# A two-layer diffusion backbone on one core: the adaLN rows and columns of the first stage issued one block ahead, and a residual moved within the change of layers

## The chip, the cores and the metric

The kernel runs on one core of a Trainium2 chip. The metric is the device time of one execution in microseconds (us). Engines are called as in the profile: PE is TensorE's matmul, PEld its weight load, DVE is VectorE, ACT ScalarE, POOL GpSimd, SP the engine whose queue issues the DMAs.

## The reference

512 latent tokens and 256 context tokens of width 1024 pass through two layers with an inner width of 2048. Layer 0 mixes tokens by a gated linear recurrence in both directions (five projections: q, two forget gates, v, and the gate z), layer 1 by a Fourier transform over tokens and over groups of channels. Each layer normalizes its input, scales and shifts it by columns computed from a condition vector (adaLN), and adds its result, times a gate, to the stream.

```python
def adaln(cvec, w, b):
    m = jax.nn.silu(cvec) @ w + b
    return jnp.split(m, 3, axis=-1)

def reference(x, c, ctx, c_ctx, ada_w, ada_b, norm_g, ...):
    x_lat, x_ctx = x, ctx
    for i in range(DEPTH):
        sh_l, sc_l, gt_l = adaln(c, ada_w[i], ada_b[i])
        h_lat = rms_norm(x_lat, norm_g[i]) * (1.0 + sc_l[:, None]) + sh_l[:, None]
        if i % N_MIXERS == 0:
            sh_c, sc_c, gt_c = adaln(c_ctx, ada_w[i], ada_b[i])
            h_ctx = rms_norm(x_ctx, norm_g[i]) * (1.0 + sc_c) + sh_c
            lb = hgrn_lower_bound(hg_lb_logits, j)
            y_lat, y_ctx = hgrn_mixer(h_ctx, h_lat, hg_w_in[j], lb, hg_norm_g[j], hg_w_out[j], ctx_out)
        else:
            y_lat = fourier_mixer(h_lat, ft_w_in[j], ft_w_out[j])
        x_lat = x_lat + gt_l[:, None] * y_lat
    return rms_norm(x_lat, final_g)
```

## The kernel before

All products are fp32 products made of two halves: `split` (L55 to L57) copies the rounded high half on ACT and subtracts it on DVE for the low half, and `mm3` (L95 to L97) is a triple of matmuls, high by high, high by low, low by high. `W` is the stream of weights: `W.loaded(n)` issues the DMA of weight block n (`wr`, 512 KB), `W.halves(n)` splits it into `wh` and `wl` (block 3 into `wz`). All large DMAs stand in SP's queue, in which a DMA is issued when the one eight places earlier has landed.

The first stage writes its order for PE, ACT and DVE by hand (`manual_schedule`). It goes over eight blocks d of 128 model columns:

- `ada_mm(d)` makes the adaLN rows: `rp` (L213, two weight tiles `wa`), then ACT copies them to `row` (L215).
- `ada_cols(d)` turns them into columns: `mp` (L221), then DVE makes `acol` and `bcol` (L222, L224).
- `turn(d, e)` transposes the normalized tokens into `tp` (L232), e = 0 for the latent tokens, e = 1 for the context.
- `modulate(d, e)` applies the columns to `tp`: the high half `hlh` (context `hc`) on ACT (L238), the full value `h32` on ACT (L241) or DVE (L243), the low half `hll` (context `hc`) on DVE (L245).
- `product(j, k)` is the triple of the projection j with block k; `first` is the sum in PSUM. Projections 0 to 2 run inside the latent loop, projection 3 in the loop over the context blocks that closes the stage.
- `square` and `normalize` prepare the tokens; `lower_bounds` makes a small matmul (`lp`) for the gates; `keep_warm` issues matmuls whose result nobody reads.

Behind that stage a scheduler sets the order from the program's text: context gates `pfc` first, then the projections, the recurrence and the output projection. At the change of layers `out0_late` makes the last output matmuls (`o0a`), tile m of 128 tokens by tile; `tail0(n)` adds token tile n's residual (`res`, `x`, L771 and L772), squares and sums (L778, L780), takes the reciprocal root on POOL (`rstd`, L179 and L180), builds a diagonal matrix of it (`dg`, L787) and the normalized halves `xn` (L788, L789). `turn1(d, r)` transposes and normalizes by a matmul with `dg` (`h1t`, L795) and makes the halves `h1h` and `h1l` (L797 to L804) for token tiles 0 and 1 (r = 0) or 2 and 3 (r = 1). `table` and `channel_table` split the Fourier tables (`tab`, `dft`). Then come the first gate products `ze` and the Fourier products `hp`.

Of the kernel before, what the change touches and what calls it, by code (L numbers as in the profile page):

```python
# [16 lines left out]
KT = D // P  # L17
T = 512
NT = T // P
TC = 256  # L20
NTC = TC // P
# [6 lines left out]
def view(t, off, dims):  # L28
    return bass.AP(t.tensor, t.offset + off, [t.ap[0]] + dims)
# [3 lines left out]
def hgrn_fourier_kernel(ctx: ExitStack, tc: tile.TileContext, a):  # L33
# [15 lines left out]
    def psG(name):  # L49
        return psum("G", 2, name)  # L50
# [60 lines left out]
    def ada_load(d):  # L111
        wa[d] = []
        for j in range(2):
            h = KT // 2
            if d < 4:
                w = py.tile([P, h, 256], F32, tag=f"yp{2 * d + j}", name=f"wa{d}_{j}")
            else:
                w = p0.tile([P, h, 256], F32, name=f"wa{d}_{j}")
            nc.sync.dma_start(out=w, in_=a["ada_a"][d][:, j * h:(j + 1) * h, :])
            wa[d].append(w)  # L120
# [14 lines left out]
    def keep_warm(n, name):  # L135
        wp = psG(name)
        for j in range(n):
            pe.matmul(wp, ones_r, view(ones_r, 0, [[0, 4], [1, P]]), start=True, stop=True)
# [64 lines left out]
    def normalize(n):  # L203
        rst = rstd_of(ss[:, n:n + 1], 1, D, p0, f"x{n}")
        v.tensor_scalar(out=xs[:, n, :], in0=xs[:, n, :], scalar1=rst, scalar2=None, op0=ALU.mult)
# [3 lines left out]
    def ada_mm(d):  # L209
        rp = psM(f"rp{d}")  # L210
        for k in range(KT):
            j = 32 * (k % 4)
            pe.matmul(rp[j:j + 32, :256], spad[:, k, :], wa[d][k // 4][:, k % 4, :], start=(k < 4), stop=(k >= 4))  # L213
        row = p0.tile([P, 256], F32, tag="row", name=f"row{d}", bufs=2)
        s.activation(row, rp[:, :256], AF.Copy)  # L215
        mcol[d] = row

    def ada_cols(d):
        mp = psM(f"mp{d}")
        for h in range(2):  # L220
            pe.matmul(mp[:, h * 2:h * 2 + 2], mcol[d][:, h * P:(h + 1) * P], sel, start=True, stop=True)  # L221
        v.tensor_scalar(out=acol[:, d, :], in0=mp[:, 2:4], scalar1=bp1[:, 8 + d:9 + d],  # L222
                        scalar2=vcol[:, 48 + d:49 + d], op0=ALU.add, op1=ALU.mult)
        v.tensor_scalar(out=bcol[:, d, :], in0=mp[:, 0:2], scalar1=vcol[:, 16 + d:17 + d], scalar2=None, op0=ALU.add)  # L224
# [3 lines left out]
    def turn(d, e):  # L228
        n0, n1 = ((0, NT), (NT, NT + NTC))[e]
        tp = turned[d, e] = psG(f"tp{d}_{e}")  # L230
        for n in range(n0, n1):
            pe.transpose(tp[:, (n - n0) * P:(n - n0 + 1) * P], xs[:, n, d * P:(d + 1) * P], ident)  # L232

    def modulate(d, e):
        n0, n1, th, tl = ((0, NT, *hlat), (NT, NT + NTC, *hctx))[e]
        w = (n1 - n0) * P
        tp = turned[d, e]
        s.activation(th[d], tp[:, :w], AF.Identity, scale=acol[:, d, e:e + 1], bias=bcol[:, d, e:e + 1])  # L238
        h32 = p0.tile([P, T], F32, tag="h32", name=f"h32_{d}_{e}", bufs=2)
        if e == 0 and d % 2:  # L240
            s.activation(h32[:, :w], tp[:, :w], AF.Identity, scale=acol[:, d, e:e + 1], bias=bcol[:, d, e:e + 1])  # L241
        else:
            v.tensor_scalar(out=h32[:, :w], in0=tp[:, :w], scalar1=acol[:, d, e:e + 1], scalar2=bcol[:, d, e:e + 1],  # L243
                            op0=ALU.mult, op1=ALU.add)
        v.tensor_tensor(out=tl[d], in0=h32[:, :w], in1=th[d].bitcast(F32), op=ALU.subtract)  # L245
# [47 lines left out]
    W = Weights(specs)  # L293
    FIRST = (1, 2, 0, 3)
    with tc.manual_schedule(engines={mybir.EngineType.PE, mybir.EngineType.Activation, mybir.EngineType.DVE}):
        first = {}

        def product(j, k):
            st = FIRST[j]
            if k == 0:  # L300
                first[st] = psP(f"first{st}")
            mm3(first[st], W.parts[j][0][:, k, :], W.parts[j][1][:, k, :], hlh[:, k, :], hll[:, k, :], k == 0, k == KT - 1)

        W.loaded(0)
        ada_load(1)
        ada_load(2)
        W.loaded(1)
        ada_load(3)
        ada_load(4)
        W.loaded(2)  # L310
        for d in range(5, KT):
            ada_load(d)
        W.loaded(3)
        for n in range(NTC):
            nc.sync.dma_start(out=xs[:, NT + n, :], in_=a["ctx"][n * P:(n + 1) * P, :])
        keep_warm(24, "warm1")
        for n in range(NT):
            square(n)
        for n in range(NT):
            normalize(n)  # L320
        ada_mm(0)
        keep_warm(3, "warm2")
        todo = {2: [(0, 0), (1, 0)], 3: [(0, 1), (1, 1), (2, 0), (2, 1)]}
        for d in range(KT):
            if d > 0:
                ada_mm(d)
            if d == 5:
                lower_bounds()
            turn(d, 0)
            if d == 0:  # L330
                keep_warm(4, "warm3")
            for j, k in todo.get(d, [(j, d - 2) for j in range(3)] if d > 3 else []):
                product(j, k)
            if d == KT - 1:
                for n in range(NT, NT + NTC):
                    square(n)
            ada_cols(d)
            modulate(d, 0)
            if d < 3:
                W.halves(d)  # L340
            if d == 6:
                W.halves(3)
        for j in range(3):
            product(j, KT - 2)
        for n in range(NT, NT + NTC):
            normalize(n)
        for j in range(3):
            product(j, KT - 1)
        for d in range(2):
            turn(d, 1)  # L350
        for d in range(KT):
            modulate(d, 1)
            product(3, d)
            if d + 2 < KT:
                turn(d + 2, 1)
# [310 lines left out]
    LAST = 13  # L666
# [12 lines left out]
    def out0_step(k, y2, w, m, hf, first, last):  # L679
        c, cm = slice(hf * 512, hf * 512 + 512), slice((m % 2) * P, (m % 2) * P + P)  # L680
        mm3(acc_of(m, hf), y2[:, 0, cm], y2[:, 1, cm], w[0][:, c], w[1][:, c], first, last)
# [10 lines left out]
    def out0_late():  # L692
        for k in range(LAST, 16):
            w = W.get(at["o0", 0, k])
            for r in range(2):
                y2 = y_parts(k, r)
                for m in (2 * r, 2 * r + 1):
                    for hf in range(2):
                        out0_step(k, y2, w, m, hf, r == 1 and k == LAST, r == 0 and k == 15)
            yield  # L700
        held = []
        for k in range(LAST):
            held.append((k, y_parts(k, 1), W.get(at["o0", 1, k])))
            if k == LAST - 2:
                continue
            for m, hfs in ((2, (0, 1)), (3, (0,)), (3, (1,))) if k == LAST - 1 else ((2, (0, 1)), (3, (0, 1))):
                for kk, y2, w in held:
                    for hf in hfs:
                        out0_step(kk, y2, w, m, hf, False, kk == LAST - 1)
            held = []  # L710
            yield

# [44 lines left out]
    def table(n):  # L757
        traw = pw.tile([P, 2, NF], F32, tag="wr", name=f"traw{n}")
        nc.sync.dma_start(out=traw, in_=a["tab"][:, n])
        tab = fp.tile([P, 2, 2, NF], F32R, tag=f"tb{n}", name=f"tab{n}")  # L760
        split(tab[:, :, 0, :], tab[:, :, 1, :], traw)
        tabs.append(tab)
# [20 lines left out]
    def tail0(n, acc):  # L783
        residual(n, acc)
        r = sum_sq(ss1, n, x1[:, n, :], f"x1_{n}")
        dg[n] = fp.tile([P, P], F32, tag="dg", name=f"dg{n}", bufs=2)
        v.tensor_scalar(out=dg[n], in0=ident, scalar1=r, scalar2=None, op0=ALU.mult)  # L787
        s.activation(xn[n][0], x1[:, n, :], AF.Copy, scale=r)  # L788
        v.scalar_tensor_tensor(out=xn[n][1], in0=x1[:, n, :], scalar=r, in1=xn[n][0].bitcast(F32),  # L789
                               op0=ALU.mult, op1=ALU.subtract)  # L790
# [22 lines left out]
    def acc_row(m):  # L813
        return [acc0[m, hf] for hf in range(2)]

    for k, _ in enumerate(out0_late()):
        if k in (3, 5):
            tail0(k // 2 - 1, acc_row(k // 2 - 1))
        if 7 <= k < 15:
            turn1(k - 7, 0)  # L820
        if k in (11, 12, 13):
            table(k - 11)
    table(3)
    channel_table()
    for n in range(2, 4):
        tail0(n, acc_row(n))


    zs_of = {}
# [66 lines left out]
    for b in range(2):  # L896
        m = fp.tile([1, NG // 2, NF], F32, tag=f"tb{b}", name=f"mid{b}")
# [139 lines left out]
```

## Time and profile before

| | us |
|---|---|
| median of 3 runs | 1208.31 (1207.48 to 1209.96) |
| the profiled execution | 1207.37, of which its span 1205.6 |
| TensorE busy | 1183.0 |
| VectorE, ScalarE, GpSimd busy | 763.1, 563.7, 43.0 |
| mean granted TensorE clock | 0.995 |

Times in a profile row count from the start of the span; the first number is the start, the second the duration, and in brackets stands the idle time of that engine ahead of it and what ended it. Matmuls overlap, so the step from one row's start to the next is what a matmul costs in a row of them. In a windows row the clock behind the busy times is the one that the throttle granted, 1.00 being full.

### The profile page before, as it was taken

The page shows a single profiled execution, that of the slowest core. Times are in us where ns is not written, and L with a number is a line of the kernel's source. Part 1 is how long each engine was busy: PE and PEld are TensorE (multiplying, and loading weights), DVE is VectorE, ACT ScalarE, POOL GpSimd, SP SyncE. Part 2 cuts the span into 40 slices and gives each one's busy share as a digit, 9 for nine tenths or more (in the row PEclk, how much of TensorE's full clock was granted, in tenths as well). Part 3 has the DMA queues.
Part 4 walks back from the last instruction along what each step waited for, and adds up shares of the span by engine and source line. Part 5 has one row for each costly group of instructions (what it writes and reads, how often), then busy time and mean ns, then how long its engine had stood idle before and what let it go on. Part 6 is the DMA issues. An engine that isn't in the chain of part 4 may idle for free.

```text
span 1205.6 us, 19232 instructions
## 1 busy us (share of the span) xinstructions
PE 1183.0 (98%) x7805; PEld 1043.4 (87%) x7805; DVE 763.1 (63%) x1250; ACT 563.7 (47%) x1130; POOL 43.0 (4%) x76
## 2 busy tenths in 40 slices
PE   7899999999999999999999999999999999999997
PEld 5699899899889889989988988998888998988885
DVE  5486655575765775686457547458576856668554
ACT  4355544554454453445445455355556533333322
POOL 2100000000000000000000000000000000000000
PEclk9999999999999999999999999999999999999998
DMA  9434211122510521242121112113545313333221
GB/s 352 177 122 156 71 54 53 53 71 70 161 61 29 182 77 54 69 142 71 36 70 54 36 54 69 37 53 109 175 168 184 110 42 134 106 108 119 88 88 70
DMA packets 33674, 118.54 MB, mean 98 GB/s; under 512 B 3879, under 2 KB 4144, under 8 KB 33586
## 3 DMA queue, kind: packets, MB, share of 16 engines
q1 hardware_dynamic: 33586, 117.32, 28.6%
q8 instruction: 61, 1.00, 0.3%
q14 instruction: 27, 0.22, 0.1%
HBM read 115.20 MB, written 2.10 MB: 97 GB/s over the span
## 4 chain that ended last, share of the span: by engine, by line
PE 91%; DVE 4%; DMA 2%; ACT 1%; issue 1%; POOL 0%; SPq 0%; DVEq 0%; POOLq 0%; ACTq 0%
PE gp L584 6%; PE pq L95 4%; PE pq L97 4%; PE pq L96 4%; PE pf L95 4%; PE pf L97 4%; PE pf L96 4%; PE vps L95 4%; PE vps L96 4%; PE vps L97 4%; PE pfc L95 2%; PE pfc L96 2%; PE pfc L97 2%; PE o0a L97 2%; PE o0a L95 2%; PE o0a L96 2%
## 5 line engine op out<-in xcount | busy, mean ns | idle before, releaser
L56 ACT ACTIVATE wh<-wr 128x1024 fp32r<-128x1024 f32 x140 | 147.9, 1058 | 225.8 <-PE pq L96 88.3
L57 DVE TENSOR_TENSOR wl<-wr,wh 128x1024 fp32r<-128x1024 f32 x140 | 170.8, 1220 | 103.6 <-ACT wh L56 101.9
L592 DVE TENSOR_TENSOR z<-z,tt 128x512 f32<-128x512 f32 x192 | 124.1, 688 | 120.6 <-PE gp L584 94.4
L95 PE MATMUL pf<-hlh,wh 128*128 128x512 f32 x240 | 99.3, 414 | 0.0
L95 PE MATMUL pq<-hlh,wh 128*128 128x512 f32 x240 | 96.9, 404 | 0.0
L545 ACT ACTIVATE kk<-z 128x512 f32<-128x512 f32 x96 | 61.8, 643 | 71.8 <-DVE z L592 71.6
L97 PE MATMUL pf<-hlh,wl 128*128 128x512 f32 x240 | 94.5, 394 | 0.0
L97 PE MATMUL pq<-hlh,wl 128*128 128x512 f32 x240 | 93.9, 391 | 0.0
L96 PE MATMUL pf<-hll,wh 128*128 128x512 f32 x240 | 93.8, 391 | 0.0
L96 PE MATMUL pq<-hll,wh 128*128 128x512 f32 x240 | 93.6, 390 | 0.0
L584 PE MATMUL gp<-z,kk 128*128 128x128 f32 x640 | 86.1, 277 | 0.6 <-ACT kk L545 0.6
L584 PEld LDWEIGHTS gp<-z,kk 128*128 128x128 f32 x640 | 81.4, 191 | 4.3 <-ACT kk L545 1.5
L95 PE MATMUL pfc<-hc,wh 128*128 128x256 f32 x256 | 74.8, 292 | 0.0
L95 PE MATMUL vps<-wh,hlh 128*128 128x256 f32 x256 | 74.2, 290 | 0.0
L97 PE MATMUL vps<-wh,hll 128*128 128x256 f32 x256 | 72.5, 283 | 0.0
L96 PE MATMUL vps<-wl,hlh 128*128 128x256 f32 x256 | 72.5, 283 | 0.0
L96 PE MATMUL pfc<-hc,wh 128*128 128x256 f32 x256 | 72.4, 283 | 0.0
L97 PE MATMUL pfc<-hc,wl 128*128 128x256 f32 x256 | 72.4, 283 | 0.0
L97 PEld LDWEIGHTS pf<-hlh,wl 128*128 128x128 f32 x240 | 45.0, 188 | 10.4 <-issue 0.2
L97 PEld LDWEIGHTS pq<-hlh,wl 128*128 128x128 f32 x240 | 45.0, 188 | 9.9
L95 PEld LDWEIGHTS pf<-hlh,wh 128*128 128x128 f32 x240 | 45.2, 188 | 9.6 <-issue 1.9
L96 PEld LDWEIGHTS pf<-hll,wh 128*128 128x128 f32 x240 | 45.3, 189 | 8.1 <-issue 0.2
(270 smaller groups left out, 3013.3 us busy)
## 6 DMA issues: line engine op xcount, KB each, us to landing
wr<-hg_w SPq DMA_DIRECT2D x64, 512.0 KB, 3.6
ar<-ada_r SPq DMA_DIRECT2D x32, 512.0 KB, 3.8
wr<-ft_w SPq DMA_DIRECT2D x32, 512.0 KB, 3.6
wr<-hg_wout SPq DMA_DIRECT2D x29, 512.0 KB, 3.4
wa<-ada_a SPq DMA_DIRECT2D x16, 512.0 KB, 10.5
wr<-hg_v SPq DMA_DIRECT2D x16, 512.0 KB, 3.4
wr<-ft_wout SPq DMA_DIRECT2D x16, 512.0 KB, 3.4
xs<-x SPq DMA_DIRECT2D x4, 512.0 KB, 3.6
```

The lines of the kernel that those rows point to most:

```text
L56: s.activation(hi, src, AF.Copy)
L57: v.tensor_tensor(out=lo, in0=src, in1=hi.bitcast(F32), op=ALU.subtract)
L95: pe.matmul(out, lh, rh, start=first, stop=False)
L96: pe.matmul(out, lh, rl, start=False, stop=False)
L97: pe.matmul(out, ll, rh, start=False, stop=last)
L545: s.activation(view(kk, 0, [[2 * h, T // (2 * h)], [h, 2], [1, h]]), view(z4, 2 * T, [[2 * h, T // (2 * h)], [T + h, 2], [1, h]]), AF.Copy)
L584: pe.matmul(gp[:, n * P:(n + 1) * P], kk[:, n * P:(n + 1) * P], view(z4, n * P, dims), start=True, stop=True)
L592: v.tensor_tensor(out=za, in0=za, in1=ta, op=ALU.mult)
```

## The change

In the first stage, `ada_mm` and `ada_cols` of block d + 1 are issued in block d; the first weight block is split ahead of `ada_mm(0)`; the triples are spread in another way over the blocks; weight block 3 and the context are loaded ahead of the adaLN weights of blocks 6 and 7, split or squared in block 5 and normalized in block 6; weight block 4 is split within the context loop at d = 3; the context's `h32` of odd blocks goes to ACT. At the change of layers `tail0(2)` stands directly behind the last matmuls of token tile 2, and `tail0(3)` ahead of the tables.

```diff
--- before.py
+++ after.py
@@ -237,7 +237,7 @@
         tp = turned[d, e]
         s.activation(th[d], tp[:, :w], AF.Identity, scale=acol[:, d, e:e + 1], bias=bcol[:, d, e:e + 1])
         h32 = p0.tile([P, T], F32, tag="h32", name=f"h32_{d}_{e}", bufs=2)
-        if e == 0 and d % 2:
+        if d % 2:
             s.activation(h32[:, :w], tp[:, :w], AF.Identity, scale=acol[:, d, e:e + 1], bias=bcol[:, d, e:e + 1])
         else:
             v.tensor_scalar(out=h32[:, :w], in0=tp[:, :w], scalar1=acol[:, d, e:e + 1], scalar2=bcol[:, d, e:e + 1],
@@ -308,48 +308,54 @@
         ada_load(3)
         ada_load(4)
         W.loaded(2)
-        for d in range(5, KT):
-            ada_load(d)
+        ada_load(5)
         W.loaded(3)
         for n in range(NTC):
             nc.sync.dma_start(out=xs[:, NT + n, :], in_=a["ctx"][n * P:(n + 1) * P, :])
+        for d in range(6, KT):
+            ada_load(d)
         keep_warm(24, "warm1")
         for n in range(NT):
             square(n)
         for n in range(NT):
             normalize(n)
+        W.halves(0)
         ada_mm(0)
         keep_warm(3, "warm2")
-        todo = {2: [(0, 0), (1, 0)], 3: [(0, 1), (1, 1), (2, 0), (2, 1)]}
+        ada_cols(0)
+        todo = {2: [(0, 0), (0, 1)], 3: [(1, 0), (1, 1), (0, 2)], 4: [(2, 0), (1, 2), (0, 3), (1, 3)],
+                5: [(2, 1), (2, 2), (0, 4), (1, 4)], 6: [(2, 3), (2, 4), (0, 5), (1, 5)],
+                7: [(2, 5), (0, 6), (1, 6)]}
         for d in range(KT):
-            if d > 0:
-                ada_mm(d)
+            turn(d, 0)
+            modulate(d, 0)
+            if d == 0:
+                keep_warm(4, "warm3")
+            if d in (1, 2):
+                W.halves(d)
+            if d + 1 < KT:
+                ada_mm(d + 1)
             if d == 5:
                 lower_bounds()
-            turn(d, 0)
-            if d == 0:
-                keep_warm(4, "warm3")
-            for j, k in todo.get(d, [(j, d - 2) for j in range(3)] if d > 3 else []):
-                product(j, k)
-            if d == KT - 1:
+                W.halves(3)
                 for n in range(NT, NT + NTC):
                     square(n)
-            ada_cols(d)
-            modulate(d, 0)
-            if d < 3:
-                W.halves(d)
             if d == 6:
-                W.halves(3)
-        for j in range(3):
-            product(j, KT - 2)
-        for n in range(NT, NT + NTC):
-            normalize(n)
+                for n in range(NT, NT + NTC):
+                    normalize(n)
+            for j, k in todo.get(d, []):
+                product(j, k)
+            if d + 1 < KT:
+                ada_cols(d + 1)
+        product(2, KT - 2)
         for j in range(3):
             product(j, KT - 1)
         for d in range(2):
             turn(d, 1)
         for d in range(KT):
             modulate(d, 1)
+            if d == 3:
+                W.halves(4)
             product(3, d)
             if d + 2 < KT:
                 turn(d + 2, 1)
@@ -707,6 +713,8 @@
                 for kk, y2, w in held:
                     for hf in hfs:
                         out0_step(kk, y2, w, m, hf, False, kk == LAST - 1)
+                if k == LAST - 1 and m == 2:
+                    tail0(2, acc_row(2))
             held = []
             yield
 
@@ -820,10 +828,9 @@
             turn1(k - 7, 0)
         if k in (11, 12, 13):
             table(k - 11)
+    tail0(3, acc_row(3))
     table(3)
     channel_table()
-    for n in range(2, 4):
-        tail0(n, acc_row(n))
 
 
     zs_of = {}
```

On PE, in blocks 2 and 3 of the first stage (rp, mp and tp carry the block's number; `first1` is projection 0, `first2` projection 1), before:

```order
L232 MATMUL tp2_0_303<-ident_73,xs_79 128x128 x4
L95 MATMUL first1_308<-hlh_129,wh0_259 128x512
L96 MATMUL first1_308<-hll_130,wh0_259 128x512
L97 MATMUL first1_308<-hlh_129,wl0_260 128x512
L95 MATMUL first2_312<-hlh_129,wh1_288 128x512
L96 MATMUL first2_312<-hll_130,wh1_288 128x512
L97 MATMUL first2_312<-hlh_129,wl1_289 128x512
L221 MATMUL mp2_316<-sel_115,row2_301 128x2 x2
L213 MATMUL rp3_329<-wa3_0_154,spad_121 32x256 x4
L213 MATMUL rp3_329<-wa3_1_156,spad_121 32x256 x4
L232 MATMUL tp3_0_340<-ident_73,xs_79 128x128 x4
L95 MATMUL first1_308<-hlh_129,wh0_259 128x512
```

and now:

```order
L221 MATMUL mp2_303<-sel_115,row2_301 128x2 x2
L232 MATMUL tp2_0_308<-ident_73,xs_79 128x128 x4
L213 MATMUL rp3_321<-wa3_0_154,spad_121 32x256 x4
L213 MATMUL rp3_321<-wa3_1_156,spad_121 32x256 x4
L95 MATMUL first1_332<-hlh_129,wh0_225 128x512
L96 MATMUL first1_332<-hll_130,wh0_225 128x512
L97 MATMUL first1_332<-hlh_129,wl0_226 128x512
L95 MATMUL first1_332<-hlh_129,wh0_225 128x512
L96 MATMUL first1_332<-hll_130,wh0_225 128x512
L97 MATMUL first1_332<-hlh_129,wl0_226 128x512
L221 MATMUL mp3_339<-sel_115,row3_330 128x2 x2
L232 MATMUL tp3_0_344<-ident_73,xs_79 128x128 x4
```

The columns mp2 stand ahead of the transposes of block 2 and rp3 directly behind them; between rp3 and mp3, which needs row3, there are two triples now, where there were the transposes of block 3 and four triples (the listing of before ends with the first row of these).

On ACT, at the end of the first stage from block 7 to the context blocks (`hc00` and `hc01` are the context's halves; the last number of h32 is e), before:

```order
L238 ACTIVATE hlh_129<-tp7_0_488,bcol_136,acol_135 128x512
L241 ACTIVATE h32_7_0_510<-tp7_0_488,bcol_136,acol_135 128x512
L56 ACTIVATE wh4_714<-wr4_683 128x1024
L238 ACTIVATE hc00_131<-tp0_1_539,bcol_136,acol_135 128x256
L238 ACTIVATE hc00_131<-tp1_1_542,bcol_136,acol_135 128x256
L238 ACTIVATE hc00_131<-tp2_1_553,bcol_136,acol_135 128x256
L238 ACTIVATE hc00_131<-tp3_1_563,bcol_136,acol_135 128x256
L238 ACTIVATE hc01_132<-tp4_1_573,bcol_136,acol_135 128x256
```

and now:

```order
L238 ACTIVATE hlh_129<-tp7_0_509,bcol_136,acol_135 128x512
L241 ACTIVATE h32_7_0_515<-tp7_0_509,bcol_136,acol_135 128x512
L238 ACTIVATE hc00_131<-tp0_1_539,bcol_136,acol_135 128x256
L238 ACTIVATE hc00_131<-tp1_1_542,bcol_136,acol_135 128x256
L241 ACTIVATE h32_1_1_557<-tp1_1_542,bcol_136,acol_135 128x256
L238 ACTIVATE hc00_131<-tp2_1_553,bcol_136,acol_135 128x256
L238 ACTIVATE hc00_131<-tp3_1_563,bcol_136,acol_135 128x256
L241 ACTIVATE h32_3_1_577<-tp3_1_563,bcol_136,acol_135 128x256
L56 ACTIVATE wh4_582<-wr4_580 128x1024
```

The split of weight block 4 moved from ahead of all context blocks to behind the fourth, and the odd blocks' h32 stand among the hc.

On DVE, at the change of layers (res2 and res3 are the residuals of token tiles 2 and 3, wl110 and wl111 the low halves of the next weights, h1l the low half of block 6 or 7), before:

```order
L57 TENSOR_TENSOR tab2_8749<-traw2_8747,tab2_8749 128x2x258
L57 TENSOR_TENSOR wl110_8849<-wr110_8759,wh110_8848 128x1024
L57 TENSOR_TENSOR wl111_8853<-wr111_8768,wh111_8852 128x1024
L804 TENSOR_TENSOR h1l_8301<-h132_7_0_8798,h1h_8300 128x256
L57 TENSOR_TENSOR tab3_8803<-traw3_8801,tab3_8803 128x2x258
L771 TENSOR_TENSOR res2_0_8810<-o0a2_0_8331,gate0_633 128x512
L771 TENSOR_TENSOR res2_1_8813<-o0a2_1_8335,gate0_633 128x512
L57 TENSOR_TENSOR dft_8306<-draw_8806,dft_8306 128x512
L772 TENSOR_TENSOR x1_8290<-x1_8290,res2_0_8810 128x512
L772 TENSOR_TENSOR x1_8290<-x1_8290,res2_1_8813 128x512
L57 TENSOR_TENSOR wml_9359<-wm_9356,wmh_9358 128x8x8
L771 TENSOR_TENSOR res3_0_8829<-o0a3_0_8339,gate0_633 128x512
```

and now:

```order
L57 TENSOR_TENSOR tab2_8749<-traw2_8747,tab2_8749 128x2x258
L779 TENSOR_TENSOR res2_0_8782<-o0a2_0_8331,gate0_639 128x512
L779 TENSOR_TENSOR res2_1_8785<-o0a2_1_8335,gate0_639 128x512
L780 TENSOR_TENSOR x1_8290<-x1_8290,res2_0_8782 128x512
L780 TENSOR_TENSOR x1_8290<-x1_8290,res2_1_8785 128x512
L57 TENSOR_TENSOR wl110_8849<-wr110_8759,wh110_8848 128x1024
L788 TENSOR_TENSOR x1_2t_8792<-ss1_8291 128x1
L779 TENSOR_TENSOR res3_0_8820<-o0a3_0_8339,gate0_639 128x512
L795 TENSOR_SCALAR dg2_8797<-ident_73,rstd_x1_2_8794 128x128
L812 TENSOR_TENSOR h1l_8301<-h132_7_0_8817,h1h_8300 128x256
L780 TENSOR_TENSOR x1_8290<-x1_8290,res3_0_8820 128x512
L797 SCALAR_TENSOR_TENSOR xn2_1_8297<-x1_8290,rstd_x1_2_8794,xn2_0_8296 128x1024
```

Residual 2 stands directly behind tab2 and ahead of wl110; residual 3, the diagonal matrix dg2 and xn2 stand ahead of tab3, and wl111 behind tab3 and dft, five rows past the end of this piece.

## The prediction

> **What bounds the kernel now.** I read the busy table and the chain that ended last first, then TensorE's waits, then the windows with their granted clock, then the timelines of the two places that the change touches.
>
> ```profile
> PE 1183.0 (98%) x7805; PEld 1043.4 (87%) x7805; DVE 763.1 (63%) x1250; ACT 563.7 (47%) x1130; POOL 43.0 (4%) x76
> PE 91%; DVE 4%; DMA 2%; ACT 1%; issue 1%; POOL 0%; SPq 0%; DVEq 0%; POOLq 0%; ACTq 0%
> ```
>
> TensorE is busy for 98% of the span and carries 91% of the chain. The change leaves its 5897 program rows as they are, so it can only win TensorE's waits, or time at a lower clock. The waits:
>
> ```profile
> engine line waited for: us in total, times, longest us
> PE first L96 <- DVE hll L245: 1.6, 1, 1.6
> PE tp L232 <- DVE h L243: 1.5, 1, 1.5
> PE first L95 <- ACT wh L56: 1.4, 1, 1.4
> PE h1t L795 <- DVE dg L787: 1.3, 1, 1.3
> PE mp L221 <- ACT row L215: 1.0, 1, 1.0
> PE ze L96 <- DVE h1l L804: 0.6, 1, 0.6
> PE ze L95 <- ACT h1h L797: 0.3, 1, 0.3
> PE hp L97 <- DVE xn L789: 0.2, 1, 0.2
> ```
>
> The rows with rp, mp, tp and "first" are the first stage: 5.5 us. The rows h1t, ze and hp are the change of layers: 1.3 + 0.6 + 0.3 + 0.2 = 2.4 us. These are the two prizes. Now the clock (columns: busy of PE, PEld, DVE, ACT, POOL, then the granted clock):
>
> ```profile
> 21.85:25.26 3.41, 1.48 (x6) 0.61 (x5) 1.92 (x2) 2.21 (x4) 0.00 (x0) 1.00 1.04 408
> 25.26:32.09 6.83, 6.83 (x32) 4.79 (x33) 3.04 (x5) 2.11 (x3) 0.00 (x0) 0.50 1.02 409
> 32.09:65.50 33.41, 30.02 (x202) 22.48 (x200) 19.43 (x40) 14.35 (x24) 5.53 (x9) 1.00 0.40 149
> ```
>
> After a stretch with 1.48 us of TensorE work in 3.41 the clock is halved for 6.83 us, and what is done in that time takes twice as long: 3.4 us lost. So in the first stage the clock counts as much as the waits.
>
> **First stage.** The change moves no weight bytes, but puts column and row matmuls one block ahead of use. Prices of one block at full clock, from the starts on TensorE (the last row's start closes the block), and at half clock:
>
> ```profile
> 33.27 0.50 PE L221 MATMUL mp<-sel,row 128*128 128x2 f32 x4
> 33.70 1.07 PE L213 MATMUL rp<-wa,spad 128*32 128x256 f32 x16
> 34.70 0.66 PE L232 MATMUL tp<-ident,xs 128*128 128x128 f32 x4
> 35.11 0.47 PE L95 MATMUL first<-hlh,wh 128*128 128x512 f32 x1
> ...
> 37.26 0.50 PE L221 MATMUL mp<-sel,row 128*128 128x2 f32 x4
> ```
>
> Columns mp 0.43, rows rp 1.00, transposes tp 0.41, three triples 2.15, so 0.717 a triple. What the front of the stage hangs on:
>
> ```profile
> 27.95 1.06 ACT L56 ACTIVATE wh<-wr 128x1024 fp32r<-128x1024 f32 x1 [0.22 <-DMA wr<-hg_w]
> 28.91 0.37 ACT L215 ACTIVATE row<-rp 128x256 f32<-128x256 f32 x1
> ```
>
> ScalarE splits the third projection's weights when their DMA lands at 27.95, and row3 stands behind that split, in both kernels. Before, the columns that need row3 (mp3) come only after the two triples of k = 0 and four of block 3, so TensorE has work meanwhile. Now mp3 stands behind rp3 and only two triples (0,0) and (0,1): TensorE runs dry and takes mp3 at 28.91 + 0.37, about 29.35. The waits of before (1.0 for row1, 1.4 for wh1) are replaced by about 0.5 at mp1, 2.0 at mp2 (row2 now behind h and wh1) and 1.5 to 2.5 at mp3; I lay these out from the durations above, and only the end, 29.35, enters the sum.
>
> From 29.35 the work left up to the first context transpose is 5 mp (2.15), 5 tp (2.05), 4 rp (4.0), 24 - 2 = 22 triples (15.8) and a small matmul of the lower bounds (0.1): 24.1 us, so 53.45 at full clock if no wait is left. The wait for hll7 goes for this reason:
>
> ```profile
> 51.01 0.28 DVE L222 TENSOR_SCALAR acol<-mp,bp,vcol 128x2 f32<-128x2 f32 x1
> 52.99 1.43 DVE L245 TENSOR_TENSOR hll<-h,hlh 128x512 fp32r<-128x512 f32 x1 [1.58 <-ACT h L241]
> 52.95 0.93 POOL L358 CAST masks<-mraw 128x896 uint8<-128x896 f32 x1 [0.54 <-DMA mraw<-masks]
> ```
>
> From acol to the end of hll7 took 51.01 to 54.42, of which 0.7 is the slow hll beside GpSimd's cast. Behind mp7 there are now tp7 and four triples, 0.41 + 4 x 0.717 = 3.3 us, and the context squares that held acol back are two blocks earlier. If hll7 is slow again, 0.2 to 0.5 returns; I take 0.
>
> The context part in the trace:
>
> ```profile
> 56.43 0.60 PE L232 MATMUL tp<-ident,xs 128*128 128x128 f32 x4
> ...
> 59.22 0.44 PE L232 MATMUL tp<-ident,xs 128*128 128x128 f32 x2 [1.49 <-DVE h L243]
> ...
> 65.50 0.28 PE L95 MATMUL pfc<-hc,wh 128*128 128x256 f32 x1
> 57.49 1.22 DVE L57 TENSOR_TENSOR wl<-wr,wh 128x1024 fp32r<-128x1024 f32 x1 [1.74 <-ACT wh L56]
> ```
>
> It took 9.07 with a wait of 1.49, in which VectorE's h stood behind wl4. The change moves wh4 and wl4 (1.06 and 1.22) to the fourth context block and half the h32 to ScalarE. The split still stands ahead of one modulation, so I keep nearly the whole wait (1.1, between 0 and 2.3, that is wh and wl in a row) and add 0.5 where ScalarE now makes hc, hc and h for a pair of blocks: 9.2. The first matmul of the context gate (pfc) then starts at 62.65 at full clock, 2.85 before 65.50.
>
> The clock takes part of this back. These are the rows at half clock:
>
> ```profile
> 25.56 0.85 PE L221 MATMUL mp<-sel,row 128*128 128x2 f32 x4
> 26.34 1.93 PE L213 MATMUL rp<-wa,spad 128*32 128x256 f32 x16
> 28.20 1.11 PE L232 MATMUL tp<-ident,xs 128*128 128x128 f32 x4
> ```
>
> From 25.56 on TensorE did not stop, and still the clock stayed low until 32.09. In the changed kernel the stretch from 21.85 to 25.26 holds even less dense work (mp2, tp2, rp3: 1.84 us), so I take the clock as halved there again. Each us at half clock behind 29.35 costs 0.5 us. The likeliest release is the one seen, at 32.09: (32.09 - 29.35) / 2 = 1.4. First stage: -2.85 + 1.4 = -1.45, say -1.5. The bounds: 0 (no lower clock there) and 3.1 (one step of 3.41 later, 35.5).
>
> Of the moved DMAs: wr3 and the context now go ahead of wa6 and wa7. At 409 GB/s (the window above) a transfer of 512 KB takes 1.28 us, so wa6 and wa7 land 3.8 us later. The sum above has rp6 at 39 and rp7 at 44, and the DMA engines, full up to 32.09, are at a share of 0.40 behind it: 0. After pfc the next weights (wl5) have 31 matmuls of cover instead of 37 or more: +0.2 (0 to 0.6).
>
> **Change of layers.**
>
> ```profile
> 924.17 0.39 PE L95 MATMUL o0a<-wh,o0y 128*128 128x512 f32 x1
> 927.50 1.23 DVE L57 TENSOR_TENSOR wl<-wr,wh 128x1024 fp32r<-128x1024 f32 x1 [2.54 <-ACT wh L56]
> ...
> 931.88 1.28 DVE L771 TENSOR_TENSOR res<-o0a,gate 128x512 f32<-128x512 f32 x2
> 939.77 1.10 POOL L179 TENSOR_SCALAR rstd_x<-x_3t 128x1 f32<-128x1 f32 x1 [2.88 <-DVE x_3t L780]
> 941.87 0.71 PE L795 MATMUL h1t<-dg,x 128*128 128x128 f32 x4 [1.32 <-DVE dg L787]
> ```
>
> VectorE idles for 2.54 us ahead of 927.50. Residual 2 is two products and two sums, 1.28 for two, so 2.6 us: it fits the idle time almost exactly, since the row at 924.17 is tile 3's first matmul of the last batch, so that tile 2 is done with 924.3. Then wl110 follows as before, and residual 3 no longer stands behind residual 2, which took the time from 931.88: 3 to 4 us (1.28 twice, with what was between), more than the 1.32 by which dg3 was late. GpSimd's 1.10 stays. What is late next: h1l7 behind residual 3's first product (0.2), wl111, which now stands behind residual 3, tab3 and dft (0.25), and xn3 (0.35). 2.4 minus 0.8 gives -1.6; bounds 0 and -2.4. The DMA queue issues the gate-weight table later; its data is needed 10 us on.
>
> **Sum.** -1.5 + 0.2 - 1.6 = -2.9. The profiled execution took 1207.37, 0.94 under the median of 1208.31. On the median: 1205.4. A change under 0.2% (2.4 us) can't be told from none here; the border of faster is 1205.9.
>
> **Rivals.** (1) The clock is not halved behind 29.35, since the two triples before it are dense work. For it: a wait of mp2 alone is short. Against it: the halving at 25.26 came with a wait of 1.4. Then -2.85 + 0.2 - 1.6 = -4.25: 1204.1. [...] (2) The release waits for dense products. From 29.35 there come mp3, tp3 and rp4, at half clock 0.78 + 0.8 + 1.86 = 3.4, so products begin at 32.8, and the release comes a step later, 35.5: -2.85 + 3.1 + 0.2 - 1.6 = -1.15: 1207.2. For it: rows 25.56 to 28.20, gapless and narrow, released nothing. (3) At the change of layers the wait only moves, to wl111 behind residual 3 or to xn3: 0 instead of -1.6, total -1.3: 1207.0. For it: four of the table's rows wait there for four different results, of VectorE and ScalarE, whose work is not less than before. (4) The other sign: the mp, tp and rp of each block keep the load under what releases the clock, until 42.3 (two more steps). (42.33 - 29.35) / 2 = 6.5, so -2.85 + 6.5 + 0.2 - 1.6 = +2.2: 1210.5. From 37.9 on, where (t - 29.35) / 2 reaches 2.85 + 1.4, the change loses. Against it: 32.09 to 65.50 shows 1.00 throughout with that same mix. (5) All of it hides behind other waits: 1208.
>
> **How the numbers follow.** Forecast 0.32, (1) 0.20, (2) 0.23, (3) 0.12, (4) 0.09, (5) 0.04. Faster by over 0.2%: nearly all of (1), two thirds of the forecast and a little of (2) and (3): 0.45. Slower: (4) with what it spills over, 0.09. The rest, 0.46, is within 0.2%. The range reaches from 1203.0, a us beyond (1) for the bounds at the layers, to 1209.0, which takes in (2), (3) and (5); the forecast's own is 1204.4 to 1206.6.
>
> **What would show it.** Clock 0.50 from about 25.3 to 32.1, and only there before 1199; TensorE's longest waits at mp2 and mp3, none for hll7; pfc at 64.0; h1t without a wait for dg, and the waits at the layers under 1 us. The prediction is wrong if the low clock has another length, or if wl111 or h1l7 takes up a wait over 1 us.

## The result and the profile after

The changed kernel took 1201.82 us in the median of 5 runs (1199.40 to 1201.91), the kernel before 1207.90 in as many beside it (1206.62 to 1209.96): a ratio of 0.9949, interval 0.9938 to 0.9960. That is 6.1 us less, where 2.9 was forecast; the range began at 1203.0. The same kernel was timed twice more, as e12 and e15: 1201.19 (0.9942) and 1201.59 (0.9950).

The profiled execution took 1201.90 us, its span 1200.1, 5.5 less than before. TensorE's waits in it:

```profile
engine line waited for: us in total, times, longest us
PE rp L213 <- DMA wa<-ada_a: 2.5, 2, 1.7
PE mp L221 <- ACT row L215: 2.5, 3, 1.1
PE tp L232 <- ACT h L241: 0.9, 1, 0.9
PE tp L232 <- DVE h L243: 0.3, 1, 0.3
```

The rows for hll, dg, wh, wl, h1l and h1h are gone. Waits for row copies took their place in the first stage; at the change of layers no row is left. The windows, first stage first, then the middle, then from the last output matmul of layer 0 to the first output matmul of layer 1:

```profile
12.41:15.83 3.42, 1.59 (x15) 0.64 (x11) 2.28 (x4) 1.27 (x2) 1.94 (x3) 1.00 1.02 417
15.83:26.07 10.24, 9.37 (x52) 5.52 (x52) 3.96 (x8) 3.30 (x6) 0.00 (x0) 0.50 1.03 414
26.07:63.62 37.55, 35.70 (x241) 26.65 (x242) 22.05 (x44) 18.64 (x33) 5.30 (x9) 1.00 0.50 195
63.62:925.16 861.54, 860.50 (x5892) 768.33 (x5891) 550.33 (x893) 438.02 (x930) 25.23 (x38) 1.00 0.26 87
925.16:1101.57 176.41, 176.26 (x1185) 163.34 (x1184) 122.37 (x214) 69.82 (x113) 1.46 (x4) 1.00 0.32 107
```

The last two of these stretches in the kernel before:

```profile
65.50:926.66 861.16, 860.36 (x5892) 768.23 (x5891) 549.41 (x891) 438.51 (x930) 25.01 (x38) 1.00 0.26 87
926.66:1107.08 180.42, 177.74 (x1184) 163.69 (x1183) 123.50 (x216) 70.02 (x113) 2.37 (x4) 1.00 0.31 104
```

So the 5.5 us are: first stage 65.50 to 63.62, -1.88; middle 861.16 to 861.54, +0.38; change of layers and Fourier layer 180.42 to 176.41, -4.01. The last row holds the surprise: TensorE's idle time there fell from 2.68 to 0.15, but its busy time fell too, from 177.74 to 176.26, for the same matmuls. That is what a stop costs beyond its idle time, as two of them show in the kernel before:

```profile
929.61 0.28 PE L96 MATMUL ze<-h1l,wh 128*128 128x256 f32 x1
929.73 0.28 PE L97 MATMUL ze<-h1h,wl 128*128 128x256 f32 x1
930.27 0.50 PE L95 MATMUL ze<-h1h,wh 128*128 128x256 f32 x2 [0.26 <-ACT h1h L797]
...
940.26 0.29 PE L97 MATMUL hp<-tab,xn 128*128 128x258 f32 x1
941.87 0.71 PE L795 MATMUL h1t<-dg,x 128*128 128x128 f32 x4 [1.32 <-DVE dg L787]
942.73 0.39 PE L95 MATMUL hp<-tab,xn 128*128 128x258 f32 x1
```

From start to start a ze matmul takes 0.12; here it is 0.54, which is 0.42 more, while the profile names 0.26 of idle time. The matmul behind the stop then takes 0.22 instead of 0.12. (A matmul's row lasts until its modelled end, 0.28, which in a dense row lies under the next ones and at a stop does not.) The stop cost 0.52, twice what the table of waits says. The stop for dg cost 1.49 into it and 0.50 behind it (the steps are 1.61 and 0.86; in a dense row they are 0.12 and 0.36), 2.0 where the table says 1.3. Added up in this way, the stops of this stretch come to about 4.3 in the kernel before. The 0.15 of idle time that is left is one stop, for h1l7, and it costs 0.41:

```profile
928.71 0.28 PE L97 MATMUL ze<-h1h,wl 128*128 128x256 f32 x1
929.13 0.39 PE L96 MATMUL ze<-h1l,wh 128*128 128x256 f32 x1
929.36 0.28 PE L97 MATMUL ze<-h1h,wl 128*128 128x256 f32 x1
```

### The profile page after: what moved, and what is told of

Read it like the earlier page. It is cut to its first block, busy times and chain, and to the rows that moved or that the text cites. A ratio compares the mean times of both kernels' runs of the same rounds, so it can differ in the third digit from the quotient of the medians.

```text
span 1200.1 us, 19241 instructions
## 1 busy us (share of the span) xinstructions
PE 1183.0 (99%) x7805; PEld 1043.5 (87%) x7805; DVE 761.4 (63%) x1246; ACT 564.7 (47%) x1134; POOL 42.1 (4%) x76
## 4 chain that ended last, share of the span: by engine, by line
PE 92%; DVE 2%; DMA 2%; ACT 2%; issue 0%; POOL 0%; SPq 0%; DVEq 0%; POOLq 0%; ACTq 0%
PE gp L590 6%; PE pf L95 5%; PE pf L97 4%; PE pf L96 4%; PE pq L95 4%; PE pq L97 4%; PE pq L96 4%; PE vps L95 4%; PE vps L97 4%; PE vps L96 4%; PE pfc L95 2%; PE pfc L96 2%; PE pfc L97 2%; PE o1a L95 2%; PE o1a L96 2%; PE o1a L97 2%
```

## The experiments

**The two halves apart.** In e1 only the second half of the change is made:

```diff
                     for hf in hfs:
                         out0_step(kk, y2, w, m, hf, False, kk == LAST - 1)
+                if k == LAST - 1 and m == 2:
+                    tail0(2, acc_row(2))
...
+    tail0(3, acc_row(3))
     table(3)
     channel_table()
-    for n in range(2, 4):
-        tail0(n, acc_row(n))
```

> Only the change of layers (residual 2 directly behind its matmuls, residual 3 ahead of the tables); the first stage as before. Theory A (from the starts in the two traces): the stretch from the last output matmul of layer 0 to the first of layer 1 went from 180.42 to 176.41 us, so this half alone gives -4.0 on 1207.9: 1203.9, and the stretch shows 176.4. Each stop of TensorE there costs about 0.26 us more than the idle time that the profile names. Theory B (my prediction's way of counting): a stop is worth the idle time alone, 2.45 in all, so at most -2.4: 1205.5, and the other 1.6 belongs to something in the first stage that reaches this far.

> Only the first stage; the change of layers as before. Theory A: the first matmul of the context gate came 1.88 us earlier and 0.38 was given back behind it, so -1.5 on 1207.9: 1206.4. Theory B: the rest of the 6.1, -3.6: 1204.3. If both halves are independent, e1 and e2 add up to the full change (-5.5 to -6.1).

e1 took 1203.17 (ratio 0.9965, 0.9953 to 0.9977), e2, the rest of the change, 1206.01 (0.9989, 0.9980 to 0.9998), both against 1207.43: -4.3 and -1.4, together -5.7. Theory A stands: the halves add up, and the layers bring three quarters. The stretch in e1:

```profile
925.84:1102.12 176.28, 176.27 (x1184) 163.39 (x1183) 121.92 (x213) 69.69 (x113) 1.46 (x4) 1.00 0.33 107
```

4.14 less than before, with a first stage that was not touched; 2.67 of that was idle time, so 1 us of named idle time was worth 1.55 us. In e2's profile the stretch is unchanged in its order but 181.62 long, with a clock of 0.50 for 3.42 us behind the stop for dg:

```profile
938.07:941.48 3.41, 1.85 (x12) 1.24 (x10) 1.80 (x5) 1.19 (x3) 1.64 (x2) 1.00 0.35 131
941.48:944.90 3.42, 3.40 (x16) 3.41 (x17) 3.25 (x6) 1.92 (x5) 0.00 (x0) 0.50 0.00 0
```

The profile of before had the same stop without a lower clock behind it. So in one execution of the two the clock was low behind such a stop.

**Which of the two residuals.** e5 has the first stage as changed, and both residuals behind the end of the output matmuls, ahead of the tables:

```diff
-                if k == LAST - 1 and m == 2:
-                    tail0(2, acc_row(2))
...
-    tail0(3, acc_row(3))
+    for n in range(2, 4):
+        tail0(n, acc_row(n))
     table(3)
```

> The changed kernel with residual 2 taken back behind the end of the output matmuls, just ahead of residual 3 and the tables; the first stage as changed. Theory A: the place of residual 2 brings most of the gain at the layers, by two ways: it uses VectorE's idle time, and with it ScalarE gets h1h7 ahead of the weight split that waits for a DMA (in the kernel before h1h7 stood behind that split, and TensorE stopped for h1h7 and h1l7). Without it these two stops return (1.4 us from start to start) and part of the one for dg3: the stretch from the last output matmul of layer 0 to the first of layer 1 is 178 to 179 us instead of 176.4, time 1203.9. Theory B: it is enough that both residuals stand ahead of the tables: 176.4 and 1201.8.

1204.46 (0.9974, 0.9965 to 0.9983). Theory A's numbers came: the stretch is 178.89, with these waits of it left:

```profile
PE h1t L801 <- DVE dg L793: 0.7, 1, 0.7
PE ze L96 <- DVE h1l L810: 0.6, 1, 0.6
```

So of the 4.0 us, 1.5 come from taking the residuals ahead of the tables, and 2.5 from residual 2's place directly behind its matmuls. Of these 2.5, ScalarE has a third. Before, and in e5, the kernel has the halves of block 7 behind the split of wh111, which waits for a DMA; in the changed kernel they are ahead of it. The stops for h1h7 and h1l7 cost 1.2 from start to start in e5, and in the changed kernel the 0.4 above is left of them, for h1l7, which now stands behind dg2 on VectorE. ScalarE before, and after:

```profile
926.41 1.06 ACT L56 ACTIVATE wh<-wr 128x1024 fp32r<-128x1024 f32 x1 [2.18 <-PE o0a L97]
928.71 1.06 ACT L56 ACTIVATE wh<-wr 128x1024 fp32r<-128x1024 f32 x1 [1.24 <-DMA wr<-ft_w]
929.67 0.55 ACT L797 ACTIVATE h1h<-h1t,b,a 128x256 fp32r<-128x256 f32 x1
```

```profile
927.15 0.18 ACT L786 ACTIVATION_READ_ACCUMULATOR x<-x 128x1 f32 x1
927.24 0.55 ACT L805 ACTIVATE h1h<-h1t,b,a 128x256 fp32r<-128x256 f32 x1
...
930.04 1.04 ACT L56 ACTIVATE wh<-wr 128x1024 fp32r<-128x1024 f32 x1
```

h1h7 comes 2.08 behind the start of the stretch instead of 3.01 (927.24 and 929.67). The text of the change does not touch h1h7; the order that the scheduler made for ScalarE turned the two round when the residual took another place in the text.

Another part lies with GpSimd. In the kernel before, the first step of its reciprocal root for tile 3 took 1.10 (at 939.77). Here is VectorE's row at that time, then both engines in e5, then GpSimd in the changed kernel:

```profile
939.60 1.22 DVE L270 TENSOR_TENSOR eo<-wr,wr 128x1024 f32<-128x1024 f32 x1
```

```profile
937.38 0.68 DVE L57 TENSOR_TENSOR dft<-draw,dft 128x512 fp32r<-128x512 f32 x1
937.55 0.56 POOL L179 TENSOR_SCALAR rstd_x<-x_3t 128x1 f32<-128x1 f32 x1 [2.88 <-DVE x_3t L786]
```

```profile
934.63 0.19 POOL L179 TENSOR_SCALAR rstd_x<-x_3t 128x1 f32<-128x1 f32 x1 [6.21 <-DVE x_3t L788]
```

Twice it ended 0.05 behind the VectorE instruction that ran beside it, before at 940.87 and in e5 at 938.11; in the changed kernel VectorE stood idle then, and it took 0.19. As far as these rows show, 0.9 of the 1.32 by which dg3 was late came from what VectorE had next in its order; no run changed this alone.

**What sets the front of the first stage.** Three theories were open: the clock, ScalarE's row copies behind the weight splits, and the DMAs. e3 adds 12 warm-up matmuls in the waits, e4 turns two lines:

```diff
-        keep_warm(24, "warm1")
+        keep_warm(31, "warm1")
...
-        keep_warm(3, "warm2")
+        keep_warm(8, "warm2")
```

> The changed kernel with 12 more warm-up matmuls whose result nobody reads (7 in the first group, 5 behind rp0), placed where TensorE waited for DMA or for row0. Theory A: the clock was halved at 15.83 after a stretch with 1.59 us of work in 3.42; with the stretches filled it stays at 1.00, mp3 then comes when wh2 and row3 allow it (29.35 by the prediction, 30.24 measured): -0.9 on 1201.8: 1200.9. Theory B: the one execution of the changed kernel with 1199.4 at a clock of 0.998 is the one in which the clock was not halved: -2.4, all executions near 1199.4. Theory C: the front hangs on ScalarE and the DMA, not on the clock: 1201.8, same.

```diff
-            if d in (1, 2):
-                W.halves(d)
             if d + 1 < KT:
                 ada_mm(d + 1)
+            if d in (1, 2):
+                W.halves(d)
```

> The changed kernel with the row copies of blocks 2 and 3 ahead of the splits of weight blocks 1 and 2 on ScalarE (the split is issued behind the rows' matmuls instead of ahead). Theory A: the front is a chain on ScalarE in which row3 stands behind wh2 (28.73 to 29.68); without it mp2 and mp3 come 1 us each earlier and mp3 by 28 instead of 30.24, -2 on 1201.8: 1199.8. Theory B: the split only moves behind the row and then holds hlh or the triples that need wh1 and wh2: same, 1201.8.

e3: 1202.22 (0.9963, 0.9951 to 0.9975), theory C's time, no different from the changed kernel. Its profile has no low clock until 23.19, and then the very wait that the prediction had worked out, the split of weight block 2 waiting for its DMA with row3 behind it:

```profile
27.85 1.06 ACT L56 ACTIVATE wh<-wr 128x1024 fp32r<-128x1024 f32 x1 [2.58 <-DMA wr<-hg_w]
28.81 0.37 ACT L215 ACTIVATE row<-rp 128x256 f32<-128x256 f32 x1
```

mp3 came at 29.23 there (29.35 forecast) and 30.24 in the changed kernel's profile, in which the low clock had made the chain up to wh2 later than the landing. e4: 1199.78 (0.9944, 0.9930 to 0.9959) against 1207.43, mp3 at 27.17 and the first matmul of the context gate at 61.07. By the medians that is theory A's size, 2 us under the changed kernel's 1201.2 to 1201.8; by the ratios, 0.9944 against 0.9942 to 0.9950, nothing is shown. Nor is all of mp3's gain the edit's: the low clock lasted 3.41 in this profile (16.05 to 19.46) and 10.24 in the changed kernel's. e7 (below), which has the same two lines, and e12, the changed kernel, have it equally long and at nearly the same place (13.74 to 20.57 and 13.94 to 20.77), with mp3 at 28.12 and 29.09: about 1 us.

Smaller pieces, each alone, changed nothing that can be told:

```diff
-        if d % 2:
+        if e == 0 and d % 2:
             s.activation(h32[:, :w], tp[:, :w], AF.Identity, ...)
```

> The changed kernel with the context's h32 all on VectorE again. Theory A: the wait of 0.89 on ScalarE's h behind wh4 goes and one on VectorE's h behind wl4 of about the same size returns: 1201.8, same, context part 9.0 to 9.2. Theory B: the move of four h32 to ScalarE is what keeps the context part at 8.98 with wl4 in it; without it 10, and 1202.8.

e6: 1200.85 (0.9943, 0.9929 to 0.9958). The wait of 0.90 is still there, now for VectorE's h: the move of the context's h32 is worth nothing that shows.

e8 takes the DMA order back (adaLN weights 5 to 7, then weight block 3 and the context).

> The changed kernel with the DMA order of before (adaLN weights 6 and 7 ahead of weight block 3 and the context). Theory A: nothing waits for either at that time, as the prediction said: 1201.8, first matmul of the context gate at 63.6 less or more the clock. Theory B: the context lands at 39.4 and its squares, which stand in block 5 ahead of the columns on VectorE and ScalarE, hold the columns of block 6: +1 to +2, 1203 to 1204.

e8: 1201.38 (0.9950, 0.9937 to 0.9962), theory A: no row waits for either.

**Going on from there.** e7 splits weight block 4 at d = 6 instead of d = 3 of the context loop, e9 takes triples forward (`todo = {1: [(0, 0)], 2: [(0, 1), (1, 0)], 3: [(1, 1), (0, 2)], ...}`), e10 fills e7's waits with matmuls, e11 is e9 with e6's line.

> The kernel with the rows first (e4), and the split of weight block 4 moved from the fourth to the seventh context block. Theory A: TensorE's wait of 0.9 in the context loop goes, since only one block is behind the split: 1198.9 against 1199.8. Theory B: the wait moves to the last block or behind pfc: 1199.8.

> The kernel of e7 (rows ahead of the weight splits, weight block 4 split at the seventh context block) with the triple (0,0) taken from block 2 to block 1, behind rp2, where TensorE waited 0.8 us for row2, and (1,0), (1,1) one block earlier. Theory A: a triple is 0.72 us, fits into that wait, and is missing behind mp3: 0.7 less than e7, 1198.5. Theory B: the triple delays mp2 by as much, since TensorE takes it in order and the halved clock makes it 1.3 us: same as e7, 1199.2.

> The kernel of e7 with 20 more warm-up matmuls whose result nobody reads (7 ahead of rp0, 5 behind rp0, 4 each behind rp1 and rp2), in the places where TensorE waits until block 2. Theory A: the clock stays at 1.00 in the whole first stage, but the front hangs on the landing of the weights and on ScalarE, so that this gives only what the low clock took from the chain from rp1 to mp3, about 1 us: 1198.2, with less spread among executions. Theory B: the low clock's place does not matter at all: 1199.2. Theory C: the added matmuls hold mp1 and mp2: slower by 1, 1200.2.

> The kernel of e9 with the context's h32 all on VectorE, as in e6. Theory A: e6 was the same as the changed kernel within what can be told, so 1198.5 like e9. Theory B: e6's 1200.85 against 1201.82 was real, because ScalarE is the engine behind which the context halves wait: 1197.6.

> The changed kernel again, beside the three above on the same chip: 1201.8, and in its profile either a low clock before block 2 and mp3 at 30 or later, or a full clock there and mp3 at 28.2 to 29.3, set by the DMA of weight block 2.

e7: 1199.19 (0.9931, 0.9919 to 0.9944); its profile has no wait for ScalarE's h in the context loop any more (0.9 in e4), but a second comparison (below) gave 1200.54, so a gain over e4 is not shown. e9: 1199.67 (0.9933), e10: 1200.37 (0.9933), e11: 1199.92 (0.9936): none has the gain that its theory A forecast. The numbers lie near theory B for e9 (1199.2) and C for e10 (1200.2), and no interval tells them from e7. e12, the changed kernel beside them, took 1201.19; in its profile the clock was low before block 2 (13.94 to 20.77), and mp3 came at 29.09, earlier than expected with a low clock. The profile of e9, in which the clock was full until 34.48, says why. The triple does fill the wait, there is none at mp2, mp3 comes at 25.76, and then TensorE stops at mp4. ScalarE, VectorE and TensorE:

```profile
28.26 1.06 ACT L56 ACTIVATE wh<-wr 128x1024 fp32r<-128x1024 f32 x1 [2.55 <-DMA wr<-hg_w]
30.99 0.78 ACT L238 ACTIVATE hlh<-tp,bcol,acol 128x512 fp32r<-128x512 f32 x1 [1.67 <-DVE bcol L224]
31.66 0.77 ACT L241 ACTIVATE h<-tp,bcol,acol 128x512 f32<-128x512 f32 x1
32.33 0.38 ACT L215 ACTIVATE row<-rp 128x256 f32<-128x256 f32 x1
```

```profile
29.35 1.23 DVE L57 TENSOR_TENSOR wl<-wr,wh 128x1024 fp32r<-128x1024 f32 x1 [2.34 <-ACT wh L56]
30.49 0.27 DVE L222 TENSOR_SCALAR acol<-mp,bp,vcol 128x2 f32<-128x2 f32 x1
```

```profile
32.76 0.61 PE L221 MATMUL mp<-sel,row 128*128 128x2 f32 x4 [3.30 <-ACT row L215]
```

Row 4 stands behind hlh3 and h3, these behind the columns of block 3, these on VectorE behind wl2, and wl2 behind the landing at 28.2. With the row taken from behind the split, the columns are still behind it. e10 stopped at the same place (1.63 us, at 32.81), and its clock fell behind that stop, from 33.61 to 37.02. The last four runs try that reading: e13 loads weight block 2 ahead of the adaLN weights of block 4, e14 moves its split,

```diff
-            if d in (1, 2):
-                W.halves(d)
+            if d in (1, 3):
+                W.halves(d // 2 + 1)
```

both on top of e9, beside the changed kernel and e7.

> The kernel of e9 with the DMA of weight block 2 ahead of the adaLN weights of block 4 instead of behind them. Theory A: in e9 TensorE stopped 3.3 us at mp4, because row4 stood behind hlh3 and h3, these behind bcol3, this behind wl2, and wl2 behind a landing at 28.2. With the landing 2.6 us earlier the stop is 0.7 to 1 and the first matmul of the context gate comes by 60.5: 1198.0. Theory B: rp4 now waits for wa4, which lands 1.3 us later, and takes the gain: 1199.5. Theory C: the low clock sets it: same as e9.

> The kernel of e9 with the split of weight block 2 moved from block 2 to block 3, behind the rows of block 4 on ScalarE and behind hll3 on VectorE. Theory A: no row and no column is queued behind that landing any more, the stop at mp4 goes: 1197.5, first matmul of the context gate by 60. Theory B: the split now holds hlh4 and the columns of block 5, and the stop moves there: 1199.5.

> The changed kernel, for comparison on the same chip: 1201.5.

> The kernel of e7 again: 1199.2, 2 us less than the changed kernel. If it is the same as the changed kernel (1201.5), e7's 1199.19 was chance.

Against 1207.09: e15, the changed kernel, 1201.59; e16 (e7) 1200.54 (0.9946, 0.9931 to 0.9962); e13 1199.42 (0.9936, 0.9919 to 0.9952); e14 1197.31 (0.9920, 0.9907 to 0.9934). In both the stop at mp4 shrank, to 0.86 and to nothing. For e13 this is not the edit's doing. e11 runs these blocks as e9 does, and its stop is 0.87: in its profile, as in e13's, the clock was low early (15.27 to 25.51, and 14.16 to 20.98), TensorE came to mp3 at 29.69 and 28.36 instead of 25.76, and by then weight block 2 had landed (in e9 at 28.2). e13's median is e9's, near theories B and C, and no matmul waited for wa4 as B has it. For e14 the edit does show, against e11 (first two rows; e14 below):

```profile
29.69 0.61 PE L221 MATMUL mp<-sel,row 128*128 128x2 f32 x4
34.26 0.61 PE L221 MATMUL mp<-sel,row 128*128 128x2 f32 x4 [0.87 <-ACT row L215]
```

```profile
28.65 0.61 PE L221 MATMUL mp<-sel,row 128*128 128x2 f32 x4
32.18 0.52 PE L221 MATMUL mp<-sel,row 128*128 128x2 f32 x4
```

From mp3 to mp4 4.57 passed in e11, and in e13, and 3.53 in e14, all at full clock behind mp3. The 1.0 is the place of wl2 ahead of the columns on VectorE: block 3's acol comes 2.30 behind mp3's start in e11 and 1.16 in e14. What a late landing adds to that, as in e9, no second profile shows.

e14 came to theory A's time. It is the best kernel of the study, 4.3 us under the changed kernel on the same chip and 9.8 under the one before, and its first matmul of the context gate comes at 60.29. It does so with a low clock as long as in the changed kernel's profile, only early:

```profile
11.81:22.05 10.24, 9.28 (x47) 4.63 (x47) 5.81 (x9) 2.49 (x4) 2.50 (x3) 0.50 1.03 416
22.05:60.29 38.24, 37.92 (x265) 27.84 (x266) 22.34 (x45) 20.20 (x35) 5.48 (x9) 1.00 0.57 220
```

What the clock itself is worth, e16 and e7 show, one kernel in two profiled executions. e16:

```profile
12.01:32.49 20.48, 19.09 (x100) 10.80 (x101) 10.19 (x18) 7.38 (x11) 2.08 (x3) 0.50 1.03 413
32.49:65.01 32.52, 32.20 (x213) 24.46 (x212) 17.72 (x37) 15.64 (x28) 5.50 (x9) 1.00 0.34 132
```

e7:

```profile
13.74:20.57 6.83, 6.43 (x31) 4.17 (x31) 3.88 (x6) 2.10 (x3) 0.27 (x1) 0.50 1.03 419
20.57:61.04 40.47, 38.63 (x273) 27.91 (x266) 22.45 (x45) 20.68 (x36) 5.30 (x9) 1.00 0.58 225
```

With the clock low until 32.49 the first matmul of the context gate came 4.0 us later, 65.01 instead of 61.04, for 13.65 us more of low clock: 0.29 us for each, not 0.5. Part of the slower work fills waits: behind the first rp row TensorE's waits for a DMA and for row copies are 2.5 us in e7 and 1.1 in e16.

## Why the prediction was wrong, and where it was right

**The change of layers: the step that failed.** "2.4 minus 0.8 gives -1.6" mis-sized both numbers. The 2.4 was the sum of the idle times in the table of waits; from start to start these stops cost 4.1 (e1), because the step into a stop and the first one behind it take longer than the idle time says. And of the 0.8 that was to be late next, at h1l7, wl111 and xn3, only h1l7's came: 0.15 of idle time, 0.41 from start to start. For h1l7 the working had looked at VectorE alone; the stops at h1h7 and h1l7 came from ScalarE's queue, where wh111 waited for a DMA ahead of h1h7, and the change turned these two round. "GpSimd's 1.10 stays" was wrong too: it became 0.19. That residual 2 would fit the idle time, and that dg3's stop would go, was right: residual 2 ran from 923.79 to 926.27. Rival (3), that the wait only moves, is out: in e1's stretch 0.01 of idle time is left.

**The first stage: size right, path half right.** -1.5 forecast, -1.88 in the profile, -1.4 in e2's median. One pair of profiles is weak ground for such a size: e1, which has the first stage of before, starts the context gate at 64.28 where before started it at 65.50, and the changed kernel starts it at 62.56 in e12 and 63.57 in e15. The chain named (landing of weight block 2, wh2, row3, mp3) set the front in e3, where the clock was full until 23.19 (wh2 at 27.85, mp3 at 29.23). In the changed kernel's own profile TensorE last waited at mp2, 0.89 for row2, and then worked without a stop up to mp3. From mp3 to the first context transpose 24.1 were counted, and 24.4 passed (30.24 to 54.64); the context part was 9.2 and is 8.98, with a wait for h on each engine (0.32 and 0.89); the wait for hll7 went. The clock was wrong: forecast low from 25.3 to 32.1, it was low from 15.83 to 26.07, before mp3, which came 0.9 later than counted, and cost nothing behind. The 1.4 of the sum was not paid, and a 0.9 that the sum did not have was: that the size came out near is in part luck. So for the clock rival (1) came true in this execution, at a price in another place. A long low clock, as rival (4) has it, did happen once, in e16, to 32.49.

**The middle.** +0.2 forecast, +0.38 in this pair. Profiles with a changed first stage have 861.14 (e6) to 862.19 (e8), and e1, with the old one, 861.56: the term can't be told from nothing.

**The offset to the median.** The sum was taken from a median of three runs, 1208.31, which lay 0.94 over the profiled execution. In five runs that median was 1207.90, and the changed kernel's profiled execution lay on its own, 1201.90 to 1201.82. This took the forecast and the range's lower end 0.4 us up, too little to matter here.

**The range.** It took every cost at the layers as bounded by the idle time, "-2.4" at most, so that no case of it reached the -4.0 that was measured.

## What to carry to other kernels

Price a stop of the busiest engine from start to start, not by the idle time that a table of waits names: here 2.7 us of named idle time were 4.1. When a dependent step is moved, look at every queue in which it now stands or no longer stands behind something that waits for a DMA; taking one instruction from behind such a wait helped only until the next one that was still behind it (e9, a stop of 3.30 at mp4). Compare a stop in two profiles only where the clock was the same up to it: e13's shrank to 0.86, and e11's to 0.87 without the edit. And when work moves into a free engine's idle time, the order that the scheduler makes of the other engines can be a part of the gain, here 0.8 of 2.5.

## What the runs showed of the hardware that was not expected

The low clock's place is not a property of the kernel. The changed kernel's three profiles have it at 15.83 to 26.07, at 13.94 to 20.77, and at 13.36 to 20.19 with 27.01 to 30.43; the lengths are 3, 2, and 2 and 1 times 3.41, and e16's 20.48 is 6 times. How long TensorE had waited did not tell where it fell: the clock fell at 15.83 behind a stretch whose longest wait was 1.11, and at 941.48 in e2 behind one of 1.33, while behind one of 1.71 (the changed kernel, 9.00 to 12.41) it stayed at 1.00. What the stretches of 3.41 us ahead of a low clock have in common is that TensorE was not busy throughout: 1.48, 1.59 and 1.85 us of work, and over all runs 1.28 (e5) to 2.13 (e4). Yet stretches of 1.55 (before, from 8.20) and 1.70 (the changed kernel, from 9.00) kept their clock, so no threshold is shown.

The release is not settled either. In the kernel before TensorE was busy for all of the 6.83 us at half clock, in the changed kernel for 9.37 of 10.24, in e16 for 19.09 of 20.48. Most of that work in the last two is adaLN rows (a weight tile of 32 columns), columns (2 columns moved through), transposes and warm-up matmuls. Whether this narrow work held the release back was not shown: no run had dense work alone there.
